# Attention scores as two full products and a 32-row leftover, a list schedule in 16 rounds, and a new order at the start

## The chip, the cores and the metric

The kernel runs on one core of a Trainium2 chip. The time is the device time of one execution in microseconds; times of several executions are given as a median with the lowest and the highest. The kernel before was timed in three executions: 736.32 us (736.19 to 736.76).

## What is computed

One transformer block on 512 tokens with 1024 features, in float32: a projection of the normed input, a gated linear attention in two directions (4 heads), a latent attention with rotary positions (8 heads), a gated merge of the two, an output projection, and a feed-forward part with a squared ReLU. The change touches the latent attention's scores. Cut to that:

```python
def mla_branch(cq, ckv, kr, positions, g_q, w_uq, g_kv, w_ukv):
    q = (rmsnorm(cq, g_q) @ w_uq).reshape(B, S, H, 64 + 32)
    q = concatenate([q[..., :64], rope(q[..., 64:], positions)], -1) * 96 ** -0.5
    kv = (rmsnorm(ckv, g_kv) @ w_ukv).reshape(B, S, H, 64 + 128)
    k_nope, v = kv[..., :64], kv[..., 64:]
    k_rope = rope(kr[:, :, None, :], positions)
    k = concatenate([k_nope, broadcast_to(k_rope, (B, S, H, 32))], -1)
    ...
    s = einsum('bhqd,bhkd->bhqk', qblk, kt)
    p = softmax(s, axis=-1)
    return einsum('bhqk,bhkv->bhqv', p, vt)
```

A query and a key of a head have 64 own features and 32 rotated ones. The rotated part of the key is the same for all heads.

## The kernel before, in words

**Products in three terms.** Each float32 operand is split into a high part, rounded to the type fp32r by a copy on ScalarE, and a low part, the difference, computed on VectorE (`split`, `split_scaled`, lines 444 to 450). A product is then three matmuls that accumulate in one bank of PSUM: high by high, high by low, low by high (`mm3`, line 439). Almost all of TensorE's work is of this kind.

**Stages.** First the normed input's first products (lines 661 to 752), written in the order in which they run. Everything behind line 1521 (`nc.keep()`) is only noted down: the gate and value projections by a seven-product scheme (class `Seven`), the linear attention (class `Linear`), the latent projections, the latent attention, the output projection and the feed-forward part. Line 2418 (`nc.flush`) puts all of this in an order and lays it down.

**The planner.** `Work.cost` (line 163) gives each instruction a price by its engine and size. `Due.order` (line 301) gives each a latest time, worked back from TensorE's instructions in the order in which they were written (`late`), and then simulates the five engines: an engine takes, of the instructions whose inputs are ready by the simulated clock, the one with the earliest `late`. TensorE may draw an instruction forward if its `late` lies within 20 us of the oldest one left. Transfers share a bus in the simulation. The order of the start times so found is the order on each engine's queue; each engine works through its queue strictly in this order. Buffers come from rings: `u2` (24 of 128x512), `u4` (30 of 128x2x512), and two rings of four PSUM banks, "mm" and "at".

**The start.** `gvec` holds the gains, biases and rotary constants as columns; it is loaded from GpSimd's queue (line 482). x, already transposed, comes in eight slices on SyncE's queue, and with each a slice of the first weights, the first of these on ScalarE's queue (lines 664 to 672). TensorE runs 11 matmuls on ones (line 675) before it has data. For each slice k, x is scaled by a column of gvec and split, the weights are split, and `first_with(k)` runs 12 matmuls: weights' high by x's high for four banks, weights' low by x's high, weights' high by x's low. For k = 0 the weights' high part is copied on VectorE. Line 750 pins all of this in program order; `gla_gain` (lines 751 and 752), which scales eight columns of gvec, stands behind that line and isn't pinned.

**The scores.** For a pair of heads, `up_units` (line 1382) loads the weights, fills rows 64 to 95 of the tile q with the rotated queries by four transfers from SyncE's queue, and computes rows 0 to 63 (the product `uq`). A tile q is 128 x 2 x 512: index 0 of the middle is the high part, 1 the low part. The tiles `kbuf` are alike: rows 0 to 63 from `uk`, rows 64 to 95 the rotated keys, which `rotary_k` (line 1271) writes to one of four tiles and copies to the other three. The values are the products `uv`. `att_scores` (line 1437) then runs, for a head and a tile of 128 queries, `mm3` over rows 0 to 95 into a bank of the ring "at", then the row maximum on VectorE and the exponential on ScalarE. `att_flip` transposes the normalised rows (`tp`) and splits them (`pT`), and `att_values` multiplies with the values (`av`). A loop over 32 tiles with lags runs these, and starts the next pair's `up_units` some steps ahead.

In the profile nearly every instruction has line 232, the one in `Script.lay` that issues it, so groups are told apart by the names of the tiles: `s` is the scores, `first` the first products, `mb` and `ab` the feed-forward part.

Of the kernel before, what the change touches and what calls it, by code (L numbers as in the profile page):

```python
# [141 lines left out]
class Work:  # L142
# [20 lines left out]
    def cost(self):  # L163
# [85 lines left out]
class Due:  # L249
# [51 lines left out]
    def order(self):  # L301
# [24 lines left out]
        for i in reversed(line):  # L326
            for j in after[i]:
                if eng[i] != "tensor" or eng[j] != "tensor":
                    late[j] = min(late[j], late[i] - cost[j] - lands[j] - todo[j].bytes / 2e5)
        free = {e: 0.0 for e in Script.ENGINES}  # L330
        free["tensor"] = self.head
# [5 lines left out]
        table = 1  # L337
        self.idle = 0.0
        for _ in range(n):
# [27 lines left out]
            if e == "tensor":  # L367
                taken[i] = True
                while pe and taken[pe[-1]]:
                    pe.pop()  # L370
                open_[e].remove(i)
                self.idle += t - free[e]
            else:
                open_[e].remove(i)
# [13 lines left out]
        out = sorted(range(n), key=lambda i: (begun[i], i))  # L388
        return out


@with_exitstack
def tile_block(ctx: ExitStack, tc: tile.TileContext, t, out: bass.AP):
# [42 lines left out]
    def raw(x):  # L436
        return x.bitcast(F32)
# [259 lines left out]
    for k in range(KD):  # L697
        wh, wl = (vh[k // 2][x][:, k % 2, :] for x in range(2))
        if k == 0:
            nc.vector.tensor_copy(wh, vraw[k])  # L700
            split_scaled(xT[k][:, 0, :], xT[k][:, 1, :], xraw[k], gmix[:, k : k + 1])
            nc.vector.tensor_tensor(wl, vraw[k], raw(wh), op=ALU.subtract)
        else:
            split_scaled(xT[k][:, 0, :], xT[k][:, 1, :], xraw[k], gmix[:, k : k + 1])
            split(wh, wl, vraw[k])
        if k < 6:
            first_with(k)
        if k:
            sq = add_square(k - 1, sq)
    sq = add_square(KD - 1, sq)  # L710
    x_tot = feature_sums(sq, "x")
    at = traced()
# [37 lines left out]
    in_program_order(fixed, None, nc.last)  # L750
    gla_gain = one([P, 8], F32, "gla_gain")
    nc.vector.tensor_scalar(gla_gain, gvec[:, V_GLA : V_GLA + 8], 0.25, None, op0=ALU.mult)


# [516 lines left out]
    def rotary_k():  # L1271
# [5 lines left out]
        nc.vector.tensor_tensor(kr[r], kr[r], kswap[r], op=ALU.add)  # L1277
        res = []
        for b in range(4):
            kb = u4(f"kbuf{b}")  # L1280
            if b == 0:
                split(kb[r, 0, :], kb[r, 1, :], kr[r])
            else:
                nc.sync.dma_start(raw(kb[r]), raw(res[0][r]))
            res.append(kb)
        return res

# [94 lines left out]
    def up_units(pr):  # L1382
# [49 lines left out]
        for i in range(2):  # L1432
            heads[2 * pr + i] = (qs[i], kbuf[2 * (pr % 2) + i], vs, slice(i * MV, (i + 1) * MV))

    probs, pTs, avs, tots = {}, {}, {}, {}

    def att_scores(head, qt):
        q, kb, _, _ = heads[head]
        tok = slice(qt * P, (qt + 1) * P)
        acc = ps("at", f"s{head}{qt}")  # L1440
        d = slice(0, NOPE + ROPE)
        mm3(acc, q[d, 0, tok], q[d, 1, tok], kb[d, 0, :], kb[d, 1, :], True, True)
        top = sm("top", 1)
# [39 lines left out]
    def att_values(head, half):  # L1483
        if head < MH - 1:
# [3 lines left out]
            hi, lo = pTs.pop((head, half))  # L1488
            _, _, vs, c = heads[head]
            for k in range(2):  # L1490
# [8 lines left out]
        hi, lo = pTs.pop((head, half))  # L1499
        _, _, vs, c = heads[head]  # L1500
        for k in range(NT):
# [155 lines left out]
    cq = cq_.normed()  # L1657
    kbuf = rotary_k()
    zb = proj_begin(w_in, C_ZB + 7 * P, "zb7")
# [787 lines left out]
```

## Time and profile before

| What | us |
|---|---|
| Median of three executions | 736.32 |
| The profiled execution's own time | 736.38 |
| Its span, from the first to the last instruction | 734.7 |
| TensorE busy in it | 725.5 |
| VectorE busy | 605.0 |
| ScalarE busy | 515.9 |

In the profile PE is TensorE's matmuls, PEld its weight loads, DVE is VectorE, ACT is ScalarE, POOL is GpSimd, and SP is SyncE, which here only issues transfers (SPq, ACTq and POOLq are the issues on the three queues). A row of the timeline has the start, the length, the engine, the source line, the operation and the tiles (out<-in), the count, and in brackets the idle time of the engine before it and what ended this. A matmul's length is the time that it takes to pass through the array; the next one starts well before it ends, so the rate is read from starts.

### The profile page before, as it was taken

The numbers are of one execution on the slowest core, as the hardware profiler recorded it, in microseconds if no ns is written. First come the engines' busy times: TensorE is split into PE (matmuls) and PEld (weight loads), VectorE is DVE, ScalarE is ACT, GpSimd is POOL, SyncE is SP. The second block draws the span as 40 slices with busy tenths as digits, with TensorE's granted clock in tenths as the row PEclk, the third lists the DMA queues.
The fourth block names the chain that finished last, engine by engine and source line by source line (L and its number), as shares of the span: only waits on it lengthen the run. The fifth ranks groups of instructions, "written<-read, shape, count | busy, mean of one in ns | idle before, by whom it ended". The sixth has DMA issues, their size and how long they took to land.

```text
span 734.7 us, 11376 instructions
## 1 busy us (share of the span) xinstructions
PE 725.5 (99%) x4130; PEld 634.9 (86%) x4130; DVE 605.0 (82%) x959; ACT 515.9 (70%) x863; POOL 201.8 (27%) x208
## 2 busy tenths in 40 slices
PE   8999999999999999999999999999999999999996
PEld 7888888888898888888888999889988998889985
DVE  6694776759999769997989899968895789778885
ACT  7574666659999657989865799637764587448744
POOL 1133031301111215037843421322132212212433
PEclk9999999999999999999999999999999999999999
DMA  9969896652312214339997889989989997998993
GB/s 312 332 144 166 214 201 114 116 116 57 87 45 71 34 54 93 73 94 247 263 266 113 192 193 252 184 190 245 194 188 200 222 211 179 217 222 197 193 164 115
DMA packets 105049, 124.37 MB, mean 169 GB/s; under 512 B 16176, under 2 KB 68416, under 8 KB 104992
## 3 DMA queue, kind: packets, MB, share of 16 engines
q0 software_dynamic: 33024, 51.14, 41.8%
q1 hardware_dynamic: 71680, 71.97, 32.1%
q8 instruction: 32, 0.52, 0.3%
q10 hardware_dynamic: 288, 0.52, 0.2%
q14 instruction: 25, 0.20, 0.1%
HBM read 119.95 MB, written 2.10 MB: 166 GB/s over the span
## 4 chain that ended last, share of the span: by engine, by line
PE 96%; ACT 1%; POOL 1%; issue 1%; DMA 1%; DVE 0%; POOLq 0%; DVEq 0%; ACTq 0%
PE mb L232 24%; PE ab L232 18%; PE zb L232 4%; PE s L232 3%; PE av L232 3%; PE wox L232 3%; PE gvx L232 3%; PE zax L232 3%; PE grx L232 3%; PE first L232 3%; PE cq L232 2%; PE gq L232 2%; PE gk L232 2%; PE tp L232 2%; PE uv L232 2%; PE gvz L232 2%
## 5 line engine op out<-in xcount | busy, mean ns | idle before, releaser
L232 POOL DMA_DIRECT2D ms<-in_w_ff x37 | 47.4, 1383 | 103.2 <-DVE hl1l L232 33.6
L232 POOL DMA_DIRECT2D w1s<-in_w_ff x19 | 25.2, 1327 | 86.3 <-DVE hl0l L232 30.2
L232 DVE TENSOR_TENSOR h<-h,ab 128x512 f32<-128x512 f32 x48 | 31.9, 683 | 10.3 <-PE ab L232 10.3
L232 ACT ACTIVATE row<-row 128x512 f32<-128x512 f32 x56 | 35.0, 626 | 5.7 <-DVE row L232 4.8
L232 PE MATMUL s<-kbuf,q 96*128 96x512 f32 x96 | 29.0, 411 | 0.0
L232 PE MATMUL av<-pT,v 128*128 128x512 f32 (+1 forms) x108 | 28.1, 382 | 0.0
L232 PE MATMUL mb<-four,hl0h 128*128 128x256 f32 x144 | 26.4, 283 | 0.0
L232 ACT ACTIVATE e<-s,top 128x512 f32<-128x512 f32 x32 | 21.9, 687 | 3.9 <-DVE top L232 3.7
L232 DVE TENSOR_TENSOR pT<-tp,pT 128x512 fp32r<-128x512 f32 x32 | 21.7, 683 | 3.5 <-ACT pT L232 3.1
L232 ACT ACTIVATE row<-mb 128x512 f32<-128x512 f32 x30 | 17.6, 586 | 9.7 <-PE mb L232 9.5
L232 PE MATMUL mb<-four,hl3h 128*128 128x256 f32 x128 | 23.4, 283 | 0.0
L232 PEld LDWEIGHTS mb<-four,hl0h 128*128 128x128 f32 x144 | 22.8, 192 | 0.5
L232 DVE TENSOR_REDUCE top<-s 128x1 f32<-128x512 f32 x32 | 21.6, 684 | 0.6 <-PE s L232 0.3
L232 ACT ACTIVATE pT<-tp 128x512 fp32r<-128x512 f32 x32 | 19.1, 597 | 3.0 <-PE tp L232 2.4
L232 PE MATMUL mb<-four,hl0l 128*128 128x256 f32 x72 | 20.5, 284 | 0.1
L232 PEld LDWEIGHTS mb<-four,hl3h 128*128 128x128 f32 x128 | 20.2, 192 | 0.3
L232 PE MATMUL mb<-four,hl2h 128*128 128x256 f32 x112 | 20.4, 283 | 0.0
L232 PE MATMUL tp<-ident,e 128*128 128x128 f32 x128 | 20.3, 272 | 0.0
L232 PEld LDWEIGHTS av<-pT,v 128*128 128x128 f32 x108 | 17.8, 189 | 2.6
L232 PEld LDWEIGHTS s<-kbuf,q 96*128 96x128 f32 x96 | 16.6, 189 | 3.3 <-ACT e L232 0.5
L232 PEld LDWEIGHTS tp<-ident,e 128*128 128x128 f32 x128 | 15.9, 140 | 3.9 <-ACT pT L232 0.3
L232 POOL DMA_DIRECT2D zaw<-in_w_in x8 | 9.5, 1190 | 33.6 <-DVE za50l L232 18.8
(1123 smaller groups left out, 2797.2 us busy)
## 6 DMA issues: line engine op xcount, KB each, us to landing
ms<-in_w_ff POOLq DMA_DIRECT2D x37, 512.0 KB, 7.9
w1s<-in_w_ff POOLq DMA_DIRECT2D x19, 512.0 KB, 7.9
ms<-in_w_ff SPq DMA_DIRECT2D x16, 512.0 KB, 6.0
w1s<-in_w_ff SPq DMA_DIRECT2D x15, 512.0 KB, 7.1
wf0f<-in_w_ff SPq DMA_DIRECT2D x11, 512.0 KB, 6.3
wf1f<-in_w_ff SPq DMA_DIRECT2D x11, 512.0 KB, 5.5
wf2f<-in_w_ff SPq DMA_DIRECT2D x11, 512.0 KB, 5.9
w<-in_w_out POOLq DMA_DIRECT2D x10, 512.0 KB, 10.0
```

Of the source, the lines that this page charges most:

```text
L232: return call(*map(real, work.args), **{k: real(v) for k, v in work.named.items()})
```

## The change

- `Work.cost`: a matmul on 32 rows is priced at 0.12.
- `Due.order` runs the simulation (now `laid`) 16 times. After each round, for each instruction of TensorE that waited over 0.05 us, it follows the latest input back up to six steps and lets those instructions have an earlier `late` in the next round. It keeps the round whose TensorE ends first. The first round is the old rule.
- gvec is loaded from ScalarE's queue, ahead of the first slice of weights; 10 warming matmuls instead of 11; for k = 0 the weights' high part is copied in two pieces, and their low part comes ahead of x's; `gla_gain` is computed ahead of line 750, behind the squares.
- The scores. Rows 64 to 127 take what was in the low plane: index 0 of q holds the high part of the 64 own features and, below it, their low part; index 0 of kbuf holds the high part twice. Index 1 of q holds the high part again, then the rotated queries' high and low parts; index 1 of kbuf holds the keys' low part, then the rotated keys' high part twice. Two matmuls over 128 rows give all terms but one: rotated queries' high part by rotated keys' low part, 32 rows. For the even tile of a pair this takes rows 64 to 95 (of q and of the new tile `krl`, here `k_low`), for the odd one rows 96 to 127 (of a new tile `qo` and of `krl`). `att_pair` runs the six matmuls of two tiles together and takes two banks at once. The copies between rows are transfers on SyncE's queue.

```diff
+            if self.args[1].parts[1] - self.args[1].parts[0] == 32:
+                return 0.12
...
+        sooner, best = [0.0] * n, None
+        for _ in range(16):
+            begun, end, held_up = self.laid(cost, eng, lands, then, waits, [a - b for a, b in zip(late, sooner)])
+            if best is None or end < best[0]:
+                best = end, begun
+            for i, wait in held_up:
+                for _ in range(6):
+                    i = max(after[i], key=lambda j: begun[j] + cost[j] + lands[j], default=None)
+                    if i is None or eng[i] == "tensor":
+                        break
+                    sooner[i] += min(wait, 1.0)
+        return sorted(range(n), key=lambda i: (best[1][i], i))
...
-    nc.gpsimd.dma_start(gvec[:, 0 : V_CST + 2], t["columns"])
+    nc.scalar.dma_start(gvec[:, 0 : V_CST + 2], t["columns"])
...
-    for _ in range(11):
+    for _ in range(10):
...
-            nc.vector.tensor_copy(wh, vraw[k])
-            split_scaled(xT[k][:, 0, :], xT[k][:, 1, :], xraw[k], gmix[:, k : k + 1])
+            for c in (slice(0, P), slice(P, S)):
+                nc.vector.tensor_copy(wh[:, c], vraw[k][:, c])
+            hi, lo = xT[k][:, 0, :], xT[k][:, 1, :]
+            nc.scalar.activation(hi, xraw[k], AF.Copy, scale=gmix[:, k : k + 1])
             nc.vector.tensor_tensor(wl, vraw[k], raw(wh), op=ALU.subtract)
+            nc.vector.scalar_tensor_tensor(
+                lo, xraw[k], gmix[:, k : k + 1], raw(hi), op0=ALU.mult, op1=ALU.subtract
+            )
...
+        low = u2("krl", F32R)
+        again = slice(96, 128)
+        res = [u4(f"kbuf{b}") for b in range(4)]
+        first = res[0][r, 1, :]
+        split(first, low[r], kr[r])
+        nc.sync.dma_start(raw(res[0][again, 1, :]), raw(first))
+        nc.sync.dma_start(raw(low[again]), raw(low[r]))
+        for kb in res[1:]:
+            for rows in (r, again):
+                nc.sync.dma_start(raw(kb[rows, 1, :]), raw(first))
+        return res, low
...
+        odd = u2(f"qo{pr}", F32R, (P, 2, 2, P))
...
-                nc.sync.dma_start(raw(q[at : at + HALF]), raw(ro[x][h : h + HALF]))
+                rope = ro[x][h : h + HALF]
+                nc.sync.dma_start(raw(q[at : at + HALF, 1, :]), raw(rope[:, 0, :]))
+                at += ROPE
+                nc.sync.dma_start(raw(q[at : at + HALF, 1, :]), raw(rope[:, 1, :]))
+                nc.sync.dma_start(
+                    raw(odd[at : at + HALF, i]),
+                    raw(rope[:, 0, :]).rearrange("p (a b t) -> p a b t", a=2, b=2)[:, :, 1, :],
+                )
...
-            split_scaled(qs[i][0:64, 0, :], qs[i][0:64, 1, :], accq[i * 64 : i * 64 + 64, :], QK_SCALE)
+            q = qs[i]
+            split_scaled(q[0:64, 0, :], q[64:128, 0, :], accq[i * 64 : i * 64 + 64, :], QK_SCALE)
+            nc.sync.dma_start(raw(q[0:64, 1, :]), raw(q[0:64, 0, :]))
...
             split(kb[0:64, 0, :], kb[0:64, 1, :], acck[i * 64 : i * 64 + 64, :])
+            nc.sync.dma_start(raw(kb[64:128, 0, :]), raw(kb[0:64, 0, :]))
...
+    def att_pair(head, qt):
+        q, odd, kb, _, _ = heads[head]
+        toks = [slice((qt + x) * P, (qt + x + 1) * P) for x in range(2)]
+        pair = [ps("at", f"s{head}{qt + x}") for x in range(2)]
+        for x in range(2):
+            nc.tensor.matmul(pair[x], q[:, 0, toks[x]], kb[:, 0, :], start=True, stop=False)
+        for x, rows in enumerate((q[64:96, 1, toks[0]], odd[96:128, qt // 2, :])):
+            d = slice(64 + 32 * x, 96 + 32 * x)
+            nc.tensor.matmul(pair[x], rows, k_low[d], start=False, stop=False)
+        for x in range(2):
+            nc.tensor.matmul(pair[x], q[:, 1, toks[x]], kb[:, 1, :], start=False, stop=True)
+        s_pair[:] = pair
```

More of the change, by code (lines that the diff above doesn't have):

```diff
@@ L329, in order, with laid @@
                     late[j] = min(late[j], late[i] - cost[j] - lands[j] - todo[j].bytes / 2e5)
+        sooner, best = [0.0] * n, None
[10 more added lines that the diff above has]
+        return sorted(range(n), key=lambda i: (best[1][i], i))
+    def laid(self, cost, eng, lands, then, waits, late):
+        todo, n, waits, held_up = self.todo, self.n, list(waits), []
         free = {e: 0.0 for e in Script.ENGINES}
@@ L371, in order @@
                 open_[e].remove(i)
-                self.idle += t - free[e]
+                if t - free[e] > 0.05:
+                    held_up.append((i, t - free[e]))
             else:
@@ L387, in order @@
                     open_[eng[j]].append(j)
-        out = sorted(range(n), key=lambda i: (begun[i], i))
-        return out
+        return begun, free["tensor"], held_up
 @with_exitstack
@@ L710, in tile_block @@
     sq = add_square(KD - 1, sq)
+    gla_gain = one([P, 8], F32, "gla_gain")
+    nc.vector.tensor_scalar(gla_gain, gvec[:, V_GLA : V_GLA + 8], 0.25, None, op0=ALU.mult)
     x_tot = feature_sums(sq, "x")
@@ L1277, in rotary_k @@
         nc.vector.tensor_tensor(kr[r], kr[r], kswap[r], op=ALU.add)
[L1278 to L1286, printed above, removed]
+        low = u2("krl", F32R)
[9 more added lines that the diff above has]
+        return res, low
     NP = 4
@@ L1432, in up_units @@
         for i in range(2):
-            heads[2 * pr + i] = (qs[i], kbuf[2 * (pr % 2) + i], vs, slice(i * MV, (i + 1) * MV))
+            heads[2 * pr + i] = (qs[i], odd[:, i], kbuf[2 * (pr % 2) + i], vs, slice(i * MV, (i + 1) * MV))
     probs, pTs, avs, tots = {}, {}, {}, {}
-    def att_scores(head, qt):
[L1438 to L1442, printed above, removed]
+    s_pair = []
+    def att_pair(head, qt):
[10 more added lines that the diff above has]
+        s_pair[:] = pair
+    def att_scores(head, qt):
+        if qt % 2 == 0:
+            att_pair(head, qt)
+        acc = s_pair[qt % 2]
         top = sm("top", 1)
@@ L1488, in att_values @@
             hi, lo = pTs.pop((head, half))
-            _, _, vs, c = heads[head]
+            _, _, _, vs, c = heads[head]
             for k in range(2):
@@ L1499, in att_values @@
         hi, lo = pTs.pop((head, half))
-        _, _, vs, c = heads[head]
+        _, _, _, vs, c = heads[head]
         for k in range(NT):
@@ L1657, in tile_block @@
     cq = cq_.normed()
-    kbuf = rotary_k()
+    kbuf, k_low = rotary_k()
     zb = proj_begin(w_in, C_ZB + 7 * P, "zb7")
```

3 lines of the change are left out of this document (removed).

## The prediction, made before the changed kernel was run

> **What bounds the kernel now.** I read the page first: the engine totals, then who makes up the chain that ended last.
>
> ```profile
> span 734.7 us, 11376 instructions
> PE 725.5 (99%) x4130; PEld 634.9 (86%) x4130; DVE 605.0 (82%) x959; ACT 515.9 (70%) x863; POOL 201.8 (27%) x208
> PE 96%; ACT 1%; POOL 1%; issue 1%; DMA 1%; DVE 0%; POOLq 0%; DVEq 0%; ACTq 0%
> ```
>
> TensorE is busy 99% of the span and is 96% of the chain. A busy TensorE is not yet one at its best rate, so I then read the chain in order of time, whose merged rows give start, duration and count.
>
> ```profile
> 1.32 4.31 DMA gvec<-in_columns
> 7.83 15.71 PE first L232 x68
> ...
> 41.30 5.44 PE grx L232 x24
> ...
> 286.69 2.88 PE uv L232 x24
> ```
>
> In a long row a 512-column matmul takes 5.44/24 = 0.227 us and a 256-column one 2.88/24 = 0.120 us: that is the rate at which matmuls follow one another, and the currency of everything below. The chain begins with a wait for one small transfer, gvec, and from 7.83 us on it is TensorE. Next the busy time by stage (TensorE, weight load, DVE, ACT, POOL, then the granted clock): the lead-in to the attention, the attention, the output projection, a stretch of the feed-forward part.
>
> ```profile
> 280.00:293.00 13.00, 13.00 (x84) 11.88 (x83) 12.64 (x23) 8.77 (x26) 7.09 (x10) 1.00 0.50 118
> 293.00:366.00 73.00, 73.00 (x413) 61.62 (x413) 65.83 (x120) 65.74 (x143) 37.81 (x44) 1.00 0.67 169
> 366.00:420.00 54.00, 53.99 (x299) 46.59 (x298) 48.89 (x76) 35.59 (x64) 23.11 (x23) 1.00 0.84 192
> ...
> 500.00:600.00 100.00, 100.00 (x681) 93.13 (x680) 80.74 (x109) 65.27 (x90) 21.67 (x18) 1.00 0.94 209
> ```
>
> TensorE has no idle time in any of them, at full clock. So a TensorE instruction that goes away in the middle is worth its rate, as long as the other engines keep up, and in the attention these are already at 90% (65.83 and 65.74 of 73). What is lost otherwise is at the start, so that stretch comes last, by instruction.
>
> ```profile
> 0.79 0.87 SPq L232 DMA_DIRECT2D x<-in_xt  x2
> 0.82 0.39 ACTq L232 DMA_DIRECT2D vw<-in_w_first  x1
> ...
> 1.08 0.23 DVE L232 CAST ones_r<-ones 128x128 fp32r<-128x128 f32 x1
> ...
> 1.10 4.18 PE L232 MATMUL warm<-ones 128*128 128x128 f32 x22 [1.10 <-DVE ones L232]
> 1.32 0.77 POOL L232 DMA_DIRECT2D gvec<-in_columns  x1 [0.83 <-POOLq L2422]
> ...
> 5.66 0.17 DVE L232 TENSOR_SCALAR gla_gain<-gvec 128x8 f32<-128x8 f32 x1 [4.35 <-DMA gvec<-in_columns]
> 5.66 1.34 ACT L232 ACTIVATE xT<-x,gvec 128x512 fp32r<-128x512 f32 x2 [3.59 <-DMA gvec<-in_columns]
> 5.74 0.42 DVE L232 CAST first0h<-vw 128x512 fp32r<-128x512 f32 x1
> ...
> 6.43 1.21 PE L232 MATMUL first<-xT,first0h 128*128 128x512 f32 x4 [1.16 <-ACT xT L232]
> ...
> 7.08 0.69 DVE L232 TENSOR_TENSOR first0l<-vw,first0h 128x512 fp32r<-128x512 f32 x1
> ...
> 7.83 1.20 PE L232 MATMUL first<-xT,first0l 128*128 128x512 f32 x4 [0.18 <-DVE first0l L232]
> ...
> 24.35 0.16 DVE L232 TENSOR_SCALAR r_x<-xss 128x4 f32<-128x4 f32 x1 [3.32 <-PE xss L232]
> ```
>
> **The start: gvec on ScalarE's queue, the first tile's splits, gla_gain, one warm-up less.** The three transfers that the first product needs, each from issue to landing (the first two for the first of their kind alone):
>
> ```profile
> x<-in_xt SPq DMA_DIRECT2D x1, 256.0 KB, 3.8
> vw<-in_w_first ACTq DMA_DIRECT2D x1, 256.0 KB, 4.0
> ...
> gvec<-in_columns POOLq DMA_DIRECT2D x1, 19.5 KB, 4.3
> ```
>
> x lands at 0.79+3.8 = 4.6, vw at 0.82+4.0 = 4.8, gvec at 1.32+4.3 = 5.6. Both ACT (the split of x scaled by a column of gvec) and DVE (held by gla_gain, which stands ahead of the copy of vw) wait for gvec. After the change gvec is issued at 0.82 and vw 0.4 us later, behind it. A small load in front of vw on a queue of the same kind should land well before vw; vw itself slips to about 4.8+0.4 = 5.2, and x, now with less beside it, stays at 4.6. ACT's split then ends at 4.6+0.77 = 5.4 (6.43−5.66 = 0.77 from its start to the matmul). DVE copies the first 128 columns of vw from 5.2 in 0.23 (the cast of ones_r has that shape), so the first four matmuls start at about 5.5 instead of 6.43. The second four need vw's remainder: the other 384 columns are copied by 5.8 (0.42 for 512), the remainder takes 0.69, and it now goes ahead of x's: 6.5. TensorE reaches them at 5.5+4×0.27 = 6.6 (four took 1.21, of which the last one's own 0.39 overlaps what follows: 0.82/3 = 0.27 each). Before they started at 7.83, after a gap that came from the old order on DVE. I take **−1.2**. If gvec's 128 short rows hold vw up by as much again as the issue did, it is −0.8; if gvec lands at 5.6 after all, only the order on DVE is won, about −0.4. At best, with vw not slipping at all, −1.6. From there TensorE runs without a gap to 23.5 at 2.72 us per step of k (12×0.227), against three DVE passes like the 0.69 of first0l, 2.1 us, so the gain is carried on. gla_gain's 0.17 us moves into a stretch where DVE waits 3.32 us for TensorE (last row): nothing. The warm-up matmul that goes frees 4.18/11 = 0.38 us of a stretch that ends at 5.28, and the products start after that: nothing.
>
> **The scores.** Now three products of 96 rows for each tile of 128 queries, 96 in all. By start times, a block after other matmuls, and one between transposes and others:
>
> ```profile
> 292.60 0.62 PE L232 MATMUL uq<-cqhl,wq1h 128*128 128x512 f32 x2
> 293.06 2.23 PE L232 MATMUL s<-kbuf,q 96*128 96x512 f32 x9
> 295.12 0.40 PE L232 MATMUL uq<-cqhl,wq1l 128*128 128x512 f32 x1
> ...
> 302.24 0.60 PE L232 MATMUL tp<-ident,e 128*128 128x128 f32 x4
> 302.60 0.94 PE L232 MATMUL s<-kbuf,q 96*128 96x512 f32 x3
> 303.38 0.28 PE L232 MATMUL uv<-wk1h,ckvhl 128*128 128x256 f32 x1
> ...
> L232 PE MATMUL s<-kbuf,q x96: 389/395/498, 293.1 to 365.1; 96*128 96x512 f32 x96
> ```
>
> Nine follow one another in 295.12−293.06 = 2.06, 0.229 each; behind transposes three take 0.78. A pair of tiles costs 6×0.229 = 1.37 now. After, it is four products of 128 rows, 4×0.229 = 0.92 (rows cost nothing: 96 and 128 rows have the same rate here), and two of 32 rows on rows 64 to 95 and 96 to 127. No matmul on 32 rows is in this trace. Lower bound for the two: one slot, 0.229, if they run side by side. Upper bound: two slots and, at the change of rows before and after, the wait for a matmul to pass through the array, its 0.395 duration less its 0.227 slot, 0.168 each: 0.458+0.336 = 0.79. The diff prices them at 0.12 each; its other TensorE prices (512/2400+0.013 = 0.226; 0.1 for a transpose, against 0.36/4 = 0.09 in the rows) agree with the trace. The nearest row, the switch from 128 rows to 96 at 293.06, came 0.46 after two uq matmuls, so it cost nothing. I take 0.24: 16×(1.37−0.92−0.24) = **−3.4**; with half as many entries behind transposes (0.78−0.69 = 0.09 each) at best −4.8.
>
> [...]
>
> **What feeds the scores.** No instruction on ACT or DVE is added; SP gets 16 small transfers for each pair of heads instead of 4, and 8 instead of 3 for the rotary keys: 53 more, at 0.58 each some 31 us of issuing on SP between 288 and 340.
>
> ```profile
> L232 ACT ACTIVATE ro<-roa x2: 628/629/630, 287.5 to 288.0; 128x512 fp32r<-128x512 f32 x2
> L232 DVE TENSOR_TENSOR ro<-roa,ro x2: 683/688/693, 288.6 to 289.2; 128x512 fp32r<-128x512 f32 x2
> ...
> 289.28 2.46 SPq L232 DMA_DIRECT2D q<-ro  x4
> ...
> L232 SPq DMA_DIRECT2D q<-ro x16: 507/580/593, 289.3 to 326.8; - x16
> ...
> DMA to landing us min/median/max: 2.2/2.3/2.8
> ```
>
> The first head is where nothing hides them. Its rotated queries are split by 289.9; two transfers then carry them, and the first score follows at 293.06. After, the first pair of tiles needs six of them and one for the low part of the rotated keys: five more, 5×0.58 = 2.9 us later. TensorE has work that depends on no score, the second pair's projections: 7 uq and 6 uk matmuls at 0.227 and 24 uv at 0.120, 5.8 us. So TensorE is covered, but the softmax on ACT and DVE starts 2.9 us later in a stretch where they have 7 us to spare in 73, of which 3.4 go with the scores. Without that cover the price is the whole 2.9. I take **+0.4**, between 0 and 2.9. Later pairs have their projections some five tiles ahead (5×73/32 = 11 us). The buffers u2 lose one to krl and one or two to qo; priced within the same bound.
>
> **The order in 16 rounds.** It can only remove waits that exist: idle TensorE time in the windows above is 0.01 us of 240, so what is to be won is the 0.09 at such seams. The first round is the old order on the new work, and a later round is kept only where the planner's own clock says sooner. That clock can be wrong on SP's queue. I take **0**, from −1 to +2.
>
> **Sum**, against the profiled execution's 736.38 (734.7 of span and 1.7 around it; the median is 736.32, 0.06 less): 736.4−1.2−3.4+0.4 = 732.2. Some of the seams will be saved; I say **732.0**, own range 730.0 to 734.3.
>
> **Rivals.** (1) The 32-row products don't overlap but cost no more than a slot each: the pair stays at 1.37, and 736.4−1.2+0.4 = 735.6. For: each has its own weight load. Against: they sit on separate rows and banks. (2) They don't overlap and TensorE empties around them: 16×0.336 = 5.4 more, 741.0, slower. It decides as soon as the two cost more than 0.458+1.2/16 = 0.53. For: nothing but the lack of any such row; against: the free switch from 128 to 96. (3) The copies come late where SP's queue is full, the last pair of heads:
>
> ```profile
> 329.65 18.85 SPq L232 DMA_DIRECT2D w<-in_w_out  x14
> ...
> w<-in_w_out SPq DMA_DIRECT2D x14, 256.0 KB, 6.9
> ```
>
> These loads are issued one after another for 19 us and take 6.9 us to land; a copy behind them lands 6.9−2.3 = 4.6 later, and if TensorE stands that long once, 732.0+4.6 = 736.6. Against: some 11 us of lead. (4) gvec lands no sooner by the other queue, so that the first line of the sum isn't done: 732.0+0.8 = 732.8.
>
> **How the numbers follow.** Forecast 0.66, (1) 0.11, (2) 0.10, (3) 0.07, (4) 0.06. Range 730.0 to 736.9: it takes in all but (2) and the tails. This kernel's measurement can tell 0.2%, 1.5 us, from no change, so "same" is 734.8 to 737.8. Faster: the forecast, (4) and a little of the others, 0.74; same: (1) and (3) less what falls outside, 0.14; slower: (2) and overlong waits, 0.12.
>
> **What would show it.** gvec on ACT's queue, landing before 4.6; the first product at about 5.5 and its second four at 6.6; a pair of score tiles in 1.16 us from its first matmul to the next other one, with the two 32-row starts within 0.05 us of each other; no TensorE idle near 293 or 348. I am wrong if the 32-row starts lie 0.2 us or more apart, if the 128-row matmul behind them starts 0.4 us or more late, or if TensorE shows waits on DMAs into q or kbuf.

## The result, and the profile after

| | before | after |
|---|---|---|
| median of the timed executions | 736.26 us (736.17 to 736.76, 4) | 745.29 us (744.79 to 746.26, 4) |
| ratio to before, 95% interval | | 1.0123 [1.0111, 1.0135] |
| span of the profiled execution | 734.7 us | 743.1 us |
| TensorE from start to start: the 96 products of the scores | 23.9 us | 30.4 us |

The change makes the kernel 9 us slower. The forecast was 732.0 us, and the time lies outside its range. Of the page of the kernel after, these are the span, the engines' totals and the shares of the chain that ended last:

```profile
span 743.1 us, 11463 instructions
PE 734.0 (99%) x4128; PEld 632.2 (85%) x4128; DVE 607.2 (82%) x960; ACT 515.7 (69%) x863; POOL 200.5 (27%) x207
PE 90%; DVE 3%; DMA 2%; ACT 2%; issue 1%; POOL 1%; POOLq 0%; ACTq 0%; DVEq 0%
```

TensorE has two instructions fewer than before and is busy 8.5 us longer. So the time didn't go into idle TensorE: its instructions took longer. A stage table says where (columns: stretch, its length, then busy time and instructions of TensorE, weight load, DVE, ACT and POOL, granted clock, share of the DMA engines, GB/s):

```profile
293.00:366.00 73.00, 72.96 (x378) 53.66 (x378) 60.79 (x107) 59.36 (x128) 31.81 (x36) 1.00 0.68 171
```

In the same 73 us before, TensorE ran 413 instructions, now 378, at the same full clock and with hardly more idle time (0.04 us), and DVE and ACT are less busy (60.79 and 59.36 after 65.83 and 65.74). The attention is stretched, and by TensorE itself. By instruction, two stretches of TensorE's queue after (start, duration from the first start to the last end, count last):

```profile
309.52 0.63 PE L234 MATMUL s<-kbuf,q 128*128 128x512 f32 x2
310.08 0.50 PE L234 MATMUL s<-krl,q 32*128 32x512 f32 x1
310.08 0.50 PE L234 MATMUL s<-krl,qo 32*128 32x512 f32 x1
310.51 0.73 PE L234 MATMUL s<-kbuf,q 128*128 128x512 f32 x2
311.08 0.62 PE L234 MATMUL av<-pT,v 128*128 128x512 f32 x2
...
326.90 0.61 PE L234 MATMUL s<-kbuf,q 128*128 128x512 f32 x2
327.44 0.49 PE L234 MATMUL s<-krl,q 32*128 32x512 f32 x1
327.86 0.50 PE L234 MATMUL s<-kbuf,q 128*128 128x512 f32 x1
328.29 0.50 PE L234 MATMUL s<-krl,qo 32*128 32x512 f32 x1
328.72 0.50 PE L234 MATMUL s<-kbuf,q 128*128 128x512 f32 x1
329.06 0.93 PE L234 MATMUL tp<-ident,e 128*128 128x128 f32 x7
```

The two 32-row products of the pair at 310.08 start together (3 ns apart in the trace). The full product behind them starts 0.43 us later, where a slot is 0.227. That pair takes 311.08−309.52 = 1.56 us. In the pair at 326.90 the planner has laid a full product between the two, and each of them is left only 0.42 to 0.43 us after its start, as is the full product between them: 329.06−326.90 = 2.16 us. Of the 16 pairs, 8 stand together and 8 apart, so TensorE goes onto 32 rows and back 24 times. I call one such trip an excursion. Before, a pair took 23.9/16 = 1.49 on average. If these two pairs are typical, 8×(1.56−1.49)+8×(2.16−1.49) = 5.9 of the measured 6.5 us are in these two kinds of rows.

The start did what was forecast (timeline of all engines, idle time and releaser at the end):

```profile
0.79 0.41 ACTq L234 DMA_DIRECT2D gvec<-in_columns  x1
1.26 0.43 ACTq L234 DMA_DIRECT2D vw<-in_w_first  x1
...
4.12 0.72 ACT L234 ACTIVATE xT<-x,gvec 128x512 fp32r<-128x512 f32 x1 [1.60 <-DMA gvec<-in_columns]
5.28 0.50 DVE L234 CAST first0h<-vw 128x128 fp32r<-128x128 f32 x2 [3.96 <-DMA vw<-in_w_first]
...
5.65 1.17 PE L234 MATMUL first<-xT,first0h 128*128 128x512 f32 x4 [0.24 <-DVE first0h L234]
6.66 1.09 PE L234 MATMUL first<-xT,first0l 128*128 128x512 f32 x4
```

From start to start of TensorE's instructions the account is: scores +6.5, start −1.3, and +3.1 spread over other products of the attention and behind it (transposes `tp` +1.1, `mb` +0.6, the rest under 0.4 each): +8.3 of the 8.4 us by which the span grew.

### The profile page after: what moved, and what is told of

The parts are those of the page before. It is cut to its first block, busy times and chain, and to the rows that moved or that the text cites. A ratio compares the mean times of both kernels' runs of the same rounds, so it can differ in the third digit from the quotient of the medians.

```text
span 743.1 us, 11463 instructions
## 1 busy us (share of the span) xinstructions
PE 734.0 (99%) x4128; PEld 632.2 (85%) x4128; DVE 607.2 (82%) x960; ACT 515.7 (69%) x863; POOL 200.5 (27%) x207
## 4 chain that ended last, share of the span: by engine, by line
PE 90%; DVE 3%; DMA 2%; ACT 2%; issue 1%; POOL 1%; POOLq 0%; ACTq 0%; DVEq 0%
PE mb L234 23%; PE ab L234 16%; PE zb L234 4%; PE s L234 4%; PE first L234 3%; PE gvx L234 3%; PE zax L234 3%; PE grx L234 3%; PE wox L234 3%; PE av L234 3%; PE cq L234 2%; PE tp L234 2%; DMA w1s<-in_w_ff 2%; PE uv L234 2%; PE gvz L234 1%; PE ckv L234 1%
## 5 line engine op out<-in xcount | busy, mean ns | idle before, releaser
L234 DVE TENSOR_TENSOR h<-h,ab 128x512 f32<-128x512 f32 x48 | 31.6, 682 | 7.4 <-PE ab L234 7.4
L234 PE MATMUL s<-kbuf,q 128*128 128x512 f32 x64 | 25.2, 444 | 0.0
L234 DVE TENSOR_TENSOR hl1l<-ms,hl1h 128x1024 fp32r<-128x1024 f32 x12 | 14.7, 1223 | 8.1 <-ACT hl1h L234 8.1
L234 ACT ACTIVATE hl1h<-ms 128x1024 fp32r<-128x1024 f32 x12 | 12.7, 1059 | 10.3 <-PE ab L234 4.6
L234 DVE TENSOR_TENSOR hl3l<-ms,hl3h 128x1024 fp32r<-128x1024 f32 x12 | 14.7, 1222 | 6.1 <-ACT hl3h L234 6.1
```

What stands on the lines that cost most here:

```text
L234: return call(*map(real, work.args), **{k: real(v) for k, v in work.named.items()})
```

## The experiments

Two theories stood at first. One, T in the expectations: the 32-row products are slow where they stand. The other: they are cheap, and the copies (R1) or the new order (R2) make TensorE wait. Each run's ratio is to the kernel before on the same chip, whose median was 736.3 to 736.5.

### The start and the rounds alone

x1_start is the kernel before with the edits of the start only (gvec's queue, the first splits, `gla_gain`, one warm-up less). x2_start_rounds adds the 16 rounds, with the scores of before. x3_after_one_round is the kernel after with

```diff
-        for _ in range(16):
+        for _ in range(1):
```

> The kernel before with the edits at the start alone: gvec first on ScalarE's queue, 10 warming matmuls, the split order of the first slice, gla_gain pinned. Theory T (the loss is in the change of rows around the 32-row products): the start's 1.2 us are won and kept, 735.1. Rival R1 (the loss is in the copies that feed the scores): the same, 735.1. Rival R2 (the loss is in the order of the 16 rounds): the same. If it shows 736.3 the gain at the start is given back later by TensorE's other waits, and none of the three has the sum right.

> The kernel before with the start's edits and the 16 rounds, scores as before. T and R1: within 0.7 us of the start alone, 734.4 to 735.8, as the old order left only some 0.25 us of idle TensorE time in the middle. R2: about 738, the 3 us that the changed kernel lost outside of the score matmuls.

> The changed kernel with one round of the simulation instead of 16. T: the excursions onto 32 rows stay, 743 to 747, more if more of the pairs fall apart than the 8 of 16 that did. R1: 743 to 747 too. R2: about 742.

Measured: 735.55 us (735.14 to 736.04), ratio 0.9983 [0.9974, 0.9992]; 735.40 (735.08 to 735.78), 0.9984 [0.9975, 0.9993]; 745.29 (744.77 to 745.82), 1.0117 [1.0103, 1.0131]. The start gives its 1 us. The rounds give nothing that stands clear of the scatter: 0.15 us on the old scores, 0.00 on the new ones. What makes the kernel slower is in the scores' edit. x2_start_rounds is below both kernels of this case, and no run was faster.

### One excursion by itself

y4_one_on_32 is x2_start_rounds with the middle one of each tile's three products on rows 64 to 95 alone; y5_one_on_64 has it on rows 0 to 63. The count of products, the layout and the copies stay those of before. The scores lack a part of this product's rows.

```diff
-        d = slice(0, NOPE + ROPE)
-        mm3(acc, q[d, 0, tok], q[d, 1, tok], kb[d, 0, :], kb[d, 1, :], True, True)
+        d, few = slice(0, NOPE + ROPE), slice(64, 96)
+        nc.tensor.matmul(acc, q[d, 0, tok], kb[d, 0, :], start=True, stop=False)
+        nc.tensor.matmul(acc, q[few, 1, tok], kb[few, 0, :], start=False, stop=False)
+        nc.tensor.matmul(acc, q[d, 0, tok], kb[d, 1, :], start=False, stop=True)
```

> The start and the rounds with the old layout, no copies and no pairs; of each tile's three products the middle one uses only the rows 64 to 95, so the scores lack a part. 32 excursions onto 32 rows, each with one product. T: 32 x 0.31 = 9.9 us more of TensorE time than 735.4, 744 to 745.5, as each still takes its own slot. Rival (what the profile shows around the 32-row products is the wait for their operands): 735.4.

> As the kernel with one product on 32 rows (748.75), but the middle product of each tile uses the rows 0 to 63, so the scores lack a part. If what costs is leaving and entering any division of the array: 747 to 749. If only 32 rows do it: 735.4.

Measured: 748.75 us (748.42 to 749.88), 1.0170 [1.0156, 1.0183], and 747.97 (747.78 to 748.21), 1.0155 [1.0141, 1.0169]. The first is above T's range, which had 0.31 for an excursion; the rival is far off. The program differs from x2_start_rounds in the rows of 32 products and in the order of a tile's last two; the planner then lays some other instructions in another order too. 13 us come of it, 12.1 of them in the scores' time from start to start. TensorE's queue in y4_one_on_32:

```profile
303.53 0.60 PE L232 MATMUL tp<-ident,e 128*128 128x128 f32 x4
303.88 1.33 PE L232 MATMUL s<-kbuf,q 96*128 96x512 f32 x3
305.05 0.28 PE L232 MATMUL uv<-wk1h,ckvhl 128*128 128x256 f32 x1
```

Its groups of instructions, each shape apart (busy time, mean duration in ns, idle time before them):

```profile
L232 PE MATMUL s<-kbuf,q 96*128 96x512 f32 x64 | 29.6, 468 | 0.0
L232 PE MATMUL s<-kbuf,q 32*128 32x512 f32 x32 | 15.8, 495 | 0.0
```

Three products behind transposes take 305.05−303.88 = 1.17 us, where the prediction's row of before has 0.78: 0.39 for one excursion. Over all, the scores take 36.0 us from start to start and took 23.9: 12.1/32 = **0.38 us for one excursion**, and the idle time of both groups is 0.0, so the profile shows no wait for another engine there. The trace splits it into about 0.1 on going onto the rows (0.32 from the product before, or 0.41 where transposes come before that; x2_start_rounds has 0.23 and 0.32), 0.2 on leaving them (0.42 to 0.43, for 0.23) and 0.1 at the product behind that (0.34, for 0.23). 64 rows cost the same as 32 (scores 35.9 us). 96 rows cost nothing against 128: the scores take 23.9 us in x2_start_rounds and 24.0 in x4_padded below, which has 128 rows throughout.

That price gives the kernel after: 64 full products at 0.249, 24 excursions at one slot and 0.38: 15.9+24×(0.24+0.38) = 30.8 us, measured 30.4. Two kernels with other counts fit as well: x3_after_one_round, with 23, gives 30.2 for 29.9 measured, and w4_after_act below, with 25, gives 31.4 for 31.6. So going onto 32 rows and back costs time, 0.38 us here; what TensorE does in it the trace doesn't show.

### All pairs together

If the separated pairs were the whole fault, keeping the two products side by side would mend it. y3_together prices the first at nothing and the second at 0.53 and lets the first wait for all that the second needs. z1_mates_tt also lays the second right behind the first, whatever the planner would do, and has the multiply of the normalising in another form (below):

```diff
+        line = sorted(range(n), key=lambda i: (best[1][i], i))
+        for i, w in enumerate(todo):
+            if w.mate is not None:
+                line.remove(i)
+                line.insert(line.index(todo.index(w.mate)) + 1, i)
+        return line
```

> The changed kernel, with the first 32-row product made to wait for what the second needs, and the two priced 0 and 0.53, so that all 16 pairs stay together instead of 8. Theory T (each excursion onto 32 rows costs 0.1 to enter, 0.21 for the work and 0.21 to leave): 24 excursions become 16, 8 x 0.53 = 4.2 us less of TensorE time, 741 to 742.5 if the waits of the padded kernel don't grow, and above 740 in any case. Rival (the two 32-row products cost their slots only where they stand apart): 735 or less.

> The changed kernel with its two 32-row products laid down one right behind the other in all 16 pairs (priced 0 and 0.53), and VectorE's half of the normalising done by a multiply of two tensors instead of the multiply by a scalar that stood 3 to 4.4 us while GpSimd ran. Theory T: 16 excursions of 0.53 to 0.6 and 64 full products, 64 x 0.23 + 16 x 0.57 = 23.8 us for the scores, what they cost before, so 735.4 and whatever waits are left, 736 to 738.5: no gain over the start and the rounds alone even so. Rival (kept together, the leftover is as cheap as the diff prices it): 732 to 733.

Measured: 746.29 us (744.36 to 747.77), 1.0132 [1.0117, 1.0147], with 11 pairs together and 21 excursions; and 744.49 (743.47 to 746.28), 1.0112 [1.0097, 1.0128], with all 16 together (in 15 of them the two start 3 to 4 ns apart, in one 0.35 us). Both lie above what was expected of them. Even with 16 the scores take 26.9 us, not 23.9. The arithmetic is that of the last experiment: an excursion shared by two products saves one slot, 0.23 to 0.25 us, and costs 0.38. By that price the 16 pairs would take 15.9+16×(0.24+0.38) = 25.8 us, so about 2 of the 3 us come out of it and the last one doesn't. What z1_mates_tt still wins in the scores against the kernel after, 3.5 us, it loses for the most part in waits: its multiply, as told below, is held for 2.4 and 1.5 us. Here is a pair side by side in w3_mates_act, a version of z1_mates_tt told of below, whose scores take 26.5 us:

```profile
313.45 0.61 PE L234 MATMUL s<-kbuf,q 128*128 128x512 f32 x2
314.00 0.49 PE L234 MATMUL s<-krl,q 32*128 32x512 f32 x1
314.00 0.50 PE L234 MATMUL s<-krl,qo 32*128 32x512 f32 x1
314.43 0.73 PE L234 MATMUL s<-kbuf,q 128*128 128x512 f32 x2
315.00 0.63 PE L234 MATMUL uq<-cqhl,wq2h 128*128 128x512 f32 x2
```

From 313.45 to 315.00 are 1.55 us; six products in a row at 0.229 are 1.37.

### The new layout without products on 32 rows

x4_padded keeps the pairs and all copies but the one inside `krl`, but the leftover is a full 128-row product against a `krl` that is zero outside its 32 rows. y1_padded_single does the same one tile at a time, without pairs.

```diff
-        for x, rows in enumerate((q[64:96, 1, toks[0]], odd[96:128, qt // 2, :])):
-            d = slice(64 + 32 * x, 96 + 32 * x)
-            nc.tensor.matmul(pair[x], rows, k_low[d], start=False, stop=False)
+        for x in range(2):
+            nc.tensor.matmul(pair[x], q[:, 1, toks[x]], k_low, start=False, stop=False)
```

> The changed kernel with each leftover as a product over all 128 rows, the low part of the rotated keys standing in a tile that is zero elsewhere: six full products for a pair of tiles, all copies but one kept, no matmul on 32 rows. T: the score matmuls fall from 30.4 us of TensorE time to 96 x 0.235 = 22.6, and the whole to 736 to 738. R1: the copies are still there, 743 or more. R2: 741 or more.

> The padded kernel (six full products for two tiles, all copies but one) with the three products of a tile together again and one bank taken at a time. The padded kernel in pairs took 740.1, the start and the rounds alone 735.4, though the score matmuls cost TensorE the same in both: 4.7 us are waits. Theory F (the copies into q and kbuf bring the softmax late): 739 to 740.5 again. Theory B (two score tiles at once, with two banks, starve the transposes): 735 to 736.5.

Measured: 740.09 us (739.61 to 742.23), 1.0053 [1.0040, 1.0067], and 740.88 (739.71 to 742.80), 1.0064 [1.0051, 1.0076]. The scores are back at 24.0 us in the first, and still the kernels are 4.7 and 5.5 above x2_start_rounds: the layout with its copies has a price of its own, with pairs and without. x4_padded lies between what T and what its rivals gave; y1_padded_single lies just above F's range and far from B's. A view of one stretch for x2_start_rounds, for x4_padded and for y1_padded_single (columns as above):

```profile
288.00:460.00 172.00, 171.86 (x1053) 151.53 (x1053) 157.09 (x256) 140.76 (x271) 73.17 (x75) 1.00 0.80 188
```

```profile
288.00:460.00 172.00, 169.18 (x1030) 147.57 (x1029) 156.30 (x248) 136.92 (x264) 75.05 (x75) 1.00 0.81 191
```

```profile
288.00:460.00 172.00, 168.88 (x1030) 147.38 (x1029) 154.10 (x246) 135.69 (x262) 74.05 (x75) 1.00 0.80 189
```

TensorE now stands for 2.8 and 3.1 us, where it stood for 0.14. That is 2.7 and 3.0 of the 5 us by which their spans exceed that of x2_start_rounds; the rest isn't placed. In x4_padded the waits are nearly all on DVE and ACT, and one of 0.3 us is on a copy (total, times, longest):

```profile
PE av L234 <- ACT pT L234: 0.7, 1, 0.7
PE tp L234 <- DVE e L234: 0.6, 1, 0.6
PE tp L234 <- ACT e L234: 0.6, 1, 0.6
PE ab L234 <- ACT ms L234: 0.3, 1, 0.3
PE s L234 <- DMA q<-ro: 0.3, 1, 0.3
```

### Why the softmax is late: a multiply that is held

y2_old_rows_paired has the old layout with no copy added, but six products of two tiles in one block, so that only the pairing is new:

```diff
+        for n, (a, b) in enumerate(((0, 0), (0, 1), (1, 0))):
+            for x in range(2):
+                nc.tensor.matmul(pair[x], q[d, a, toks[x]], kb[d, b, :], start=n == 0, stop=n == 2)
```

> The start and the rounds, scores on 96 rows as before with no copy added, but the six matmuls of two tiles run together on two banks taken at once. F: 735 to 736. B: 739 to 740. If both this and the single padded kernel lie between, the two share the 4.7 us.

Measured: 744.00 us (743.49 to 744.58), 1.0103 [1.0090, 1.0116], 8.6 above x2_start_rounds with nothing added anywhere. That is more than either theory gave: F doesn't foresee it, and B gave 739 to 740. Its timeline, DVE and POOL around 337 us:

```profile
335.47 1.71 POOL L232 TENSOR_TENSOR glyo<-yo,ghyo 128x512 fp32r<-128x512 f32 x1
...
336.63 4.39 DVE L232 TENSOR_SCALAR e<-e,tot 128x512 f32<-128x512 f32 x1
336.72 1.15 POOL L232 TENSOR_TENSOR zo<-mx,yo 128x256 f32<-128x256 f32 x1
337.42 1.69 POOL L232 TENSOR_TENSOR gao<-mx,gao 128x512 fp32r<-128x512 f32 x1
338.67 1.13 POOL L232 TENSOR_TENSOR mx<-tb,y 128x256 f32<-128x256 f32 x1
339.36 1.12 POOL L232 TENSOR_TENSOR my<-tb,y 128x256 f32<-128x256 f32 x1
340.04 1.61 POOL L232 DMA_DIRECT2D w<-in_w_out  x1
340.95 0.67 DVE L232 TENSOR_TENSOR pT<-tp,pT 128x512 fp32r<-128x512 f32 x1
```

All sixteen of these multiplies (shortest, median and longest in ns), TensorE's longest wait, and the stages around its second stop:

```profile
L232 DVE TENSOR_SCALAR e<-e,tot x16: 475/479/4394, 296.1 to 376.0; 128x512 f32<-128x512 f32 x16
```

```profile
PE tp L232 <- DVE pT L232: 4.0, 2, 2.9
```

```profile
288.00:460.00 172.00, 167.08 (x996) 145.79 (x995) 152.52 (x241) 132.29 (x257) 71.03 (x74) 0.98 0.75 173
...
356.00:360.00 4.00, 2.05 (x13) 1.42 (x11) 3.73 (x4) 2.33 (x6) 3.92 (x5) 1.00 1.08 318
360.00:364.00 4.00, 3.06 (x10) 2.58 (x11) 3.51 (x7) 2.69 (x7) 0.32 (x2) 0.59 1.01 265
364.00:368.00 4.00, 4.00 (x14) 3.22 (x13) 3.08 (x5) 1.75 (x4) 3.92 (x5) 0.55 0.30 41
```

DVE's multiply `e<-e,tot` (the half of the normalising that `att_normalise` gives it) takes 0.479 us by its median and 4.39 at 336.63. POOL's run of elementwise work ends at 339.36+1.12 = 340.48, and the multiply at 341.02, about its own usual time later. That this run holds it is read from such coincidences, here and in w5_padded_no_odd below, for no run took POOL's work away. A second multiply there, 2.75 us long from 356.94, fits less well: it ends at 359.69, where one instruction of POOL has ended at 359.40 and the next runs. The split of `pT` behind it on DVE is late, and TensorE waits for that, here and again at 358. After the second stop TensorE's granted clock averages 0.59 and 0.55 over two stretches of 4 us (in the trace it is 0.50 from 360.8 to 367.5): (1−0.59)×3.06+(1−0.55)×4.00 = 3.1 us more, an estimate. Between 288 and 460 TensorE stands for 172−167.08 = 4.9 us, 4.8 more than in x2_start_rounds; this and these 3.1 are 7.9 of the 9.4 by which the span exceeds that of x2_start_rounds.

The next runs take the multiply away from where it is held. z3_paired_tt and z4_padded_tt (y2_old_rows_paired and x4_padded) write it in another form, which might not be held; w2_paired_act, w1_padded_act, w3_mates_act and w4_after_act (from y2_old_rows_paired, x4_padded, z1_mates_tt with the old form, and the kernel after) give it to ScalarE for the heads where POOL's run lies.

```diff
-        nc.vector.tensor_scalar(b, b, tot[:, 1:2], None, op0=ALU.mult)
+        nc.vector.tensor_tensor(b, b, tot[:, 1:2].to_broadcast([P, S]), op=ALU.mult)
```

```diff
+        if head in (4, 5, 6):
+            nc.scalar.activation(b, b, AF.Copy, scale=tot[:, 1:2])
+        else:
+            nc.vector.tensor_scalar(b, b, tot[:, 1:2], None, op0=ALU.mult)
```

> The kernel with the old rows in pairs (744.0), with VectorE's half of the normalising as a multiply of two tensors. Its profile showed two multiplies by a scalar of 4.39 and about 2.7 us where 0.48 is usual, while GpSimd ran several elementwise instructions. Theory P (VectorE's multiply by a scalar stands until GpSimd pauses, and that is the wait): 738 to 740. Rival B (the banks taken two at a time starve the transposes): 743 or more, as the new multiply is 0.2 us longer.

> The padded kernel in pairs (740.1, one multiply by a scalar of 3.9 us) with the same edit. P: 736 to 737.5. F (the copies bring the softmax late): 740 again.

> The old rows in pairs (744.0; held 6.1 us in two instructions) with the same edit. P: 736.5 to 739. B: 743 or more.

> The padded kernel in pairs (740.1), with VectorE's half of the normalising of heads 4 to 6 done on ScalarE, which GpSimd can't hold. Theory P (the instruction held on VectorE is the wait, whatever its form): 736 to 737.5, though ScalarE has 4.4 us more to do. F and B (copies, banks): 740 or more.

> The changed kernel with its two 32-row products kept together in all 16 pairs and the same edit. T with P: scores 24 us, 737 to 740. Rival (other waits of the softmax come in its place): 743 or more.

> The changed kernel with the same edit alone. T: the 24 excursions stay, 741 to 744. If the held multiply were most of the loss: 738.

| kernel | from | to | ratio to before | held on DVE, largest |
|---|---|---|---|---|
| z3_paired_tt | 744.00 | 737.63 (736.33 to 738.12) | 1.0012 [1.0004, 1.0021] | none over 1 us |
| z4_padded_tt | 740.09 | 745.87 (744.15 to 747.31) | 1.0126 [1.0110, 1.0141] | 3.6 and 2.6 us |
| w2_paired_act | 744.00 | 737.96 (737.23 to 740.12) | 1.0023 [1.0014, 1.0032] | 1.0 us |
| w1_padded_act | 740.09 | 740.77 (739.47 to 741.81) | 1.0057 [1.0045, 1.0069] | 0.8 us |
| w3_mates_act | 744.49 | 742.80 (742.48 to 743.62) | 1.0086 [1.0073, 1.0099] | 0.6 us |
| w4_after_act | 745.29 | 746.39 (745.75 to 747.73) | 1.0130 [1.0116, 1.0145] | 0.8 us |

In the paired kernel without added copies the hold and what follows from it carry most of the loss: with it gone by either way, 6.0 to 6.4 of the 8.6 us are back, and 2.2 to 2.6 stay. Each edit also gives a new order, so the two ways together bear this out better than either alone. That the form decides falls with z4_padded_tt, where the new form is held for 3.6 us (4.23 for a median of 0.68) and POOL is busy throughout 336 to 340 and 356 to 360, just where TensorE's two stops behind such multiplies begin. So each form was held in a kernel whose order puts POOL's run there. And the hold isn't the price of the copies: w1_padded_act has no long hold left and is no faster, so other waits took its place. In w3_mates_act, 742.80, the scores account for 2.6 of the 7.4 us above x2_start_rounds; the other 4.8 are about what the layout costs the padded kernels. Its time lies between what was expected by theory and rival. In the kernel after there is no long hold (its longest such multiply is 1.54 us), and w4_after_act is no faster, against what was expected: its order makes 25 excursions, with 31.6 us for the scores.

Why the multiply takes so long beside POOL's run no run shows. It isn't one instruction of POOL alone: the multiply took 4.39 us for 0.48 beside five successive ones, each of which starts before the last one ends. ACT's half of the normalising took 0.71 us at 337.46, beside the same run of POOL, for a median of 0.723 in that kernel; with heads 4 to 6 on ScalarE, its longest is 0.76 in w1_padded_act and w2_paired_act and 0.79 in w6_padded_no_odd_act below.

### The copies

What is left is the layout's price, 4.7 to 5.5 us. w5_padded_no_odd is y1_padded_single without the tiles `qo` and their 24 transfers, which padded products don't read; w6_padded_no_odd_act also has the multiply on ScalarE for heads 4 to 6.

```diff
-        odd = u2(f"qo{pr}", F32R, (P, 2, 2, P))
...
-                nc.sync.dma_start(
-                    raw(odd[at : at + HALF, i]),
-                    raw(rope[:, 0, :]).rearrange("p (a b t) -> p a b t", a=2, b=2)[:, :, 1, :],
-                )
```

> The padded products, one tile at a time as in y1_padded_single (740.88), without the tiles qo and their 24 transfers, which these products don't read. Q (the four qo buffers of the ring u2 and their transfers on SP's queue carry what is left over with the copies): 735.4 to 737.5, and the waits of TensorE on the softmax engines fall to what the order with the old scores has. R (what is left of the copies carries it: the low halves of q and kbuf, the padded krl): 739.5 to 741.5. H (the multiply held on VectorE carries it): within 1 of 740.88 if it is still held over 2 us, within 2 of 735.4 if not.

> The same, and VectorE's half of the normalising of heads 4 to 6 on ScalarE. Q: 735.4 to 738. R: 738.5 to 741.5, with waits of TensorE that lead back to a copy or to a full ring. H: 735.4 to 738, below the kernel with the multiply on VectorE by what that one is held.

Measured: 741.66 us (739.22 to 743.44), 1.0062 [1.0043, 1.0082], and 738.40 (737.59 to 739.45), 1.0025 [1.0015, 1.0034]. Q, that `qo`'s buffers and transfers carry the price, falls: without them the time is not lower. In the first of them it is no longer `e<-e,tot` that is held but a subtraction of two operands, with the same kind of POOL work beside it. Again it ends about its own usual time, 1.22 us, after that work (356.75+1.42 = 358.17, and 359.26), and TensorE waits 2.3 us:

```profile
355.12 4.14 DVE L234 TENSOR_TENSOR bo20l<-bo20f,bo20h 128x1024 fp32r<-128x1024 f32 x1
...
355.22 1.73 POOL L234 TENSOR_TENSOR glyo<-yo,ghyo 128x512 fp32r<-128x512 f32 x1
356.75 1.42 POOL L234 TENSOR_TENSOR gao<-mx,gao 128x512 fp32r<-128x512 f32 x1
```

```profile
PE av L234 <- DVE pT L234: 2.3, 1, 2.3
```

In the second the order puts that subtraction elsewhere, where it takes 1.22 us, no hold exceeds 1.2 us, and the median is 3.3 us lower. The two profiled executions, both at a mean granted clock of 0.998, differ by only 1.8 us (739.86 and 738.06): three of the five executions of w5_padded_no_odd have a mean clock of 0.995 and take 741.7 to 743.4 us. So in this order H, the hold, carries 1.8 to 3.3 of the 6.3 us above x2_start_rounds, the clock included. The 738.40 lies between H's range and R's. Of the remaining 3.0, and of what keeps w1_padded_act at 740.8 without a long hold, a part shows as waits of TensorE of 0.2 to 0.8 us, most of them on steps of the softmax. Whether the low halves' copies, the buffers of the ring `u2` or only the order bring them wasn't settled; kernels with more or fewer of these buffers weren't tried.

## Why the prediction was wrong

- **The scores, −3.4: the failed step.** It took two 32-row products for 0.24 a pair "if they run side by side", which no row of before shows, on the ground that "the switch from 128 rows to 96" cost nothing. That row can't bear it: 96 rows do cost nothing (23.9 us for the scores, 24.0 on 128 rows), and 64 and 32 rows cost 0.38 us an excursion. Side by side they do start 3 ns apart, but that saves one slot and pays 0.38. With all pairs together the scores come to 26.5 to 26.9 us, +2.6 to +3.0, not −3.4; in the kernel after they come to 30.4, +6.5.
- **How often.** Sum and rivals counted 16 excursions. The planner's price for a 32-row product, 0.12 wherever it stands, gives it no reason to keep two together, and the order has 24. That nothing holds the pair together can be read in the diff; the prediction didn't count it. This is the step from +3 to the measured +6.5.
- **The upper bound, 0.79 a pair.** A pair together takes 1.56−0.92 = 0.64, inside it; a pair apart 2.16−0.92 = 1.24, far outside, as the bound knew of one entry and one exit only.
- **Rival (2)**, "TensorE empties around them", came nearest: a loss of time at the change of rows. Its price, 0.336, an estimate from a matmul's duration less its slot, was near the measured 0.38; that TensorE empties there no trace shows. Its other half, "they don't overlap", was wrong where two stand side by side, and its count was 16, so that its 741.0 is still 4 us short. It had a chance of 0.10, with "nothing but the lack of any such row" for it. A cost that no row shows, either way, should have had more weight beside a forecast built on its absence. Rival (1), that each costs no more than a slot, falls with the 0.38 us.
- **The start, −1.2: right.** gvec landed by 4.12, the first product began at 5.65 and the second four at 6.66 (5.5 and 6.6 in the working), and the start alone gives 1.0 us.
- **The 16 rounds, 0: right** (0.15 and 0.00 us won, neither clear of the scatter).
- **What feeds the scores, +0.4 of 0 to 2.9: undersized, and sought in the wrong place.** In the kernels with the layout TensorE waits once for a copy at most, for 0.2 to 0.6 us, and in the kernel after the first score starts at 291.3, sooner than before (293.06). The layout costs 4.7 to 5.5 where no product stands on 32 rows, and 3.1 in the kernel after is outside the scores and the start; what brings it isn't settled. The working priced one late start; it didn't ask what a new order of DVE's and POOL's work costs, though it quoted both softmax engines at 90% of the stage. Rival (3), a copy late behind `w`, didn't occur; rival (4) neither.

## What to carry to other kernels

Matmuls on 32 rows among matmuls on 96 or 128, as here, are worth their slots only if enough of them share one excursion: one costs 0.38 us and a second product saves 0.23, so by these numbers two lose and three would about break even (an estimate; more than two weren't tried). Let the order's planner see what belongs side by side, or lay it down as one. Where two engines stand at 90% of a stage, as in this attention, a new order alone can be some microseconds worse (8.6 in y2_old_rows_paired), so an edit there should be tried in more than one order before its price is believed.

## What the runs showed of the hardware

- Going onto 32 or 64 rows and back cost TensorE 0.38 us beyond the slots (36.0 and 35.9 us for the scores after 23.9, with 32 excursions), although the granted clock is 1.00 from 288 to 460 in y4_one_on_32 and the idle time before these products 0.0; 96 rows cost nothing (23.9 us, and 24.0 on 128 rows).
- A DVE instruction of 0.48 us from SBUF to SBUF took 4.39 us (y2_old_rows_paired), and one of 1.22 us took 4.14 (w5_padded_no_odd), while POOL ran successive elementwise instructions; each ended about its own usual time after the last of these (0.54 and 1.09 us).
- TensorE's granted clock fell to 0.50 in the middle of three kernels. In y2_old_rows_paired this followed a stop of 2.9 us and lasted 6.8 us. In z4_padded_tt it followed two stops of 2.3 and 2.4 us and lasted 3.4 us each time:

```profile
PE tp L234 <- DVE e L234: 4.6, 2, 2.4
```

```profile
340.00:344.00 4.00, 2.62 (x10) 2.15 (x11) 3.92 (x6) 2.02 (x5) 3.87 (x5) 0.78 1.09 247
344.00:348.00 4.00, 4.00 (x24) 3.74 (x23) 2.52 (x5) 1.95 (x5) 0.00 (x0) 0.79 1.11 213
...
360.00:364.00 4.00, 2.45 (x8) 1.61 (x9) 3.63 (x6) 1.94 (x5) 1.53 (x3) 0.84 1.09 243
364.00:368.00 4.00, 4.00 (x18) 3.25 (x17) 2.75 (x5) 1.68 (x4) 1.86 (x3) 0.73 0.43 79
```

In y3_together it was 0.50 for 3.4 us from 374.5 (0.81 and 0.76 on average over 372 to 376 and 376 to 380), with no stop over 1.1 us anywhere in the attention. After the stop of 2.3 us in w5_padded_no_odd's trace it stayed at 1.00 (350 to 374). So the length of one stop doesn't decide it here, and what does is open.
